# A two-layer hybrid encoder on one core: attention values of all heads in one 512-column set, and a new order of the units and gates around them

## The chip, the cores and the metric

The kernel runs on one NeuronCore of a Trainium2 chip. The core has a matrix engine (TensorE, PE in the profile, with its weight loads listed as PEld), a vector engine (VectorE, DVE), a scalar engine (ScalarE, ACT), GpSimd (POOL) and a sync engine (SP) that here only issues DMA transfers. Matrix products accumulate in PSUM banks of 128 partitions by 512 floats; all other data of the core is in SBUF. The metric is the device time of one execution in microseconds; before the change its median over three runs is 1792.9 us.

## The reference

The input `x` has 512 tokens of 1024 features. Each of two layers normalises `x` and projects it once, with `w_in`, into everything that three token mixers need:

```
h = rmsnorm(x, norm_mix[i])
qa, ka, va, glu_in, qc, kc, vc, gates = split(h @ w_in[i])
ya = diff_attention(qa, ka, va, ...)        # 4 heads, value width 128 each: va has 512 columns
yb = conformer_conv(glu_in, ...)            # a * sigmoid(g) over 512 channels, then 31 taps, layernorm, silu
yc = neighbourhood_attention(qc, kc, vc, rpb)  # 8 heads of 64: vc has 512 columns; 8x16 windows, bias
ga, gb, gc = split(sigmoid(gates))          # 3 x 1024 columns
x = x + (ga*(ya@w_br_a) + gb*(yb@w_br_b) + gc*(yc@w_br_c)) @ w_o
x = x + (silu(rmsnorm(x)@w_ffn_gate) * (rmsnorm(x)@w_ffn_up)) @ w_ffn_down
x = x + sigmoid(rmsnorm(x)@w_ple_gate) * (p[i] @ w_ple_in)
```

A last RMS norm follows both layers. The change lies in the first half of each layer, from the projection `h @ w_in` to the merge of the three branches.

## The kernel before

**Products.** All arithmetic of the matrix engine keeps float32 accuracy by splitting each operand into a high and a low half. A product is three matmuls: high weights by high activations (L177), high weights by low activations (L178), low weights by high activations (L179). A weight block of 128 by 1024 floats (512 KB) is loaded by SP into a tile `wr`; ScalarE copies its high half into `wh` (L143) and VectorE subtracts to get the low half `wl` (L157). There are three buffers each of `wr`, `wh` and `wl`, so a block can be split only when the block three before it has been used up. A gemm (`gemm`, `proj`) multiplies one block with the eight 128-feature slices of the activations: 24 matmuls of 512 columns into one PSUM bank. PSUM is shared out as three banks `mm` for gemms, two `sc` for scores, two `tr` for transposes and one `av` for attention outputs.

**Order.** The program order of PE is written out by hand. VectorE, ScalarE and SP work through orders that the scheduler makes from priorities; each executes its own list strictly in order. Inside the hand order a small clock spreads the attention work: each product of three matmuls is a *chunk*, four chunks (12 matmuls of 512 columns) make one *stretch* (`tick`), and `later(unit, delay, gap)` starts an attention unit at the earliest `delay` stretches after now and leaves at least `gap` stretches to the next one. A unit runs in steps: its scores, two stretches later its transposes, two stretches later its products with the values, whose result is read out of the bank `av` by ScalarE and VectorE (the tiles `natten_y` for the neighbourhood attention, and the like for the differential one).

**The stage of the change.** In a layer the gemms follow as: the convolution's gated units (four pairs of a value and a gate, `glu`); neighbourhood pairs 0 to 3, each a Q and a K gemm (`natten_in`) and four units; their values (`natten_v`), a first half after pair 0 and a second half after pair 2; differential heads 0 to 3 (`diff_in`) with their values (`diff_v`) in two halves; the gates of the neighbourhood branch (`gate_c`, eight gemms, the first of them behind head 1) and two of the gates of the convolution branch (`gate_b`); the sigmoid of these ten in one block (one table load on ScalarE); then `branch_c`, two more `gate_b` and `merge_a`. In layer 0 the first gemms use activations that are not normalised yet (their result is scaled by the norm afterwards); `renorm` meanwhile writes normalised activations `hs` (the tiles `glu_h<-pre_x`, each a high half on ScalarE and a low half on VectorE, L160), and everything from the first values on uses these.

**The values.** Values come out with tokens on the partitions: 128 tokens of the activations are the stationary operand, the weights are streamed through. `values` before the change does one half of the heads: 256 columns, eight feature slices, four token tiles, three matmuls each (L572, L574, L576), which makes 96 matmuls of 256 columns into two `mm` banks with two weight blocks.

**Background work.** The 31 taps of the convolution for each of four channel tiles are single VectorE operations (`conv_z<-glu_z,pre_par,conv_z`, L160, the first of a tile L505). They are dealt out behind other work in numbers set by the table `BG` (for instance four behind each sigmoid of `merge_a`, and two behind each sum, `mergea2`).

## Time and profile before

| what | us |
|---|---|
| median of three runs | 1792.9 |
| the runs | 1792.49, 1792.9, 1795.68 |
| profiled execution, whole | 1793.18 |
| profiled execution, span of the core | 1791.4 |
| PE busy in the span | 1777.5 (99%) |
| DVE busy in the span | 1381.7 (77%) |
| ACT busy in the span | 894.0 (50%) |

The profile is of one execution. The span is the time between its first and its last instruction; 1.8 us of the execution lie around it. A line of the timeline gives start, duration, engine, source line, operation, the tile written and those read, the shape, a count, and in square brackets the time that the engine sat idle before, with what ended it. The durations of matmuls are modelled latencies that overlap, so the pace of PE is read from the starts, not from the durations. Tile names carry the stage in which they were allocated: `natten` is the neighbourhood attention, `diff` the differential one, `glu_h` the activations, `gatec`/`gateb` the gates.

### The profile page before, as it was taken

The numbers are of one execution on the slowest core, as the hardware profiler recorded it, in microseconds if no ns is written. First come the engines' busy times: TensorE is split into PE (matmuls) and PEld (weight loads), VectorE is DVE, ScalarE is ACT, GpSimd is POOL, SyncE is SP. The second block draws the span as 40 slices with busy tenths as digits, with TensorE's granted clock in tenths as the row PEclk, the third lists the DMA queues.
The fourth block names the chain that finished last, engine by engine and source line by source line (L and its number), as shares of the span: only waits on it lengthen the run. The fifth ranks groups of instructions, "written<-read, shape, count | busy, mean of one in ns | idle before, by whom it ended". The sixth has DMA issues, their size and how long they took to land. (4 is left out here: it accounts for less than half of the span.)

```text
span 1791.4 us, 27360 instructions
## 1 busy us (share of the span) xinstructions
PE 1777.5 (99%) x10404; PEld 1571.6 (88%) x10404; DVE 1381.7 (77%) x2140; ACT 894.0 (50%) x1497; POOL 63.5 (4%) x102
## 2 busy tenths in 40 slices
PE   9999999999999999999999999999999999999998
PEld 7888888888899899898878888888888998998987
DVE  7888887897877577577787878878878775765776
ACT  5466555325565245255545755553256652542544
POOL 0000000000000000000000000000000100000000
PEclk9999999999999999999999999999999999999999
DMA  5666561335646456253437655523364662663432
GB/s 200 174 185 169 143 163 43 102 89 167 209 143 186 140 150 195 79 139 121 159 117 191 187 152 160 130 63 103 98 190 148 194 178 84 190 179 111 116 109 95
DMA packets 98387, 257.56 MB, mean 144 GB/s; under 512 B 12880, under 2 KB 17616, under 8 KB 98256
## 3 DMA queue, kind: packets, MB, share of 16 engines
q1 hardware_dynamic: 90912, 231.00, 41.5%
q0 software_dynamic: 6336, 23.07, 7.1%
q8 instruction: 82, 1.34, 0.3%
q10 hardware_dynamic: 1008, 1.75, 0.3%
q14 instruction: 49, 0.40, 0.1%
HBM read 216.44 MB, written 7.86 MB: 125 GB/s over the span
## 5 line engine op out<-in xcount | busy, mean ns | idle before, releaser
L143 ACT ACTIVATE ffn_wh<-ffn_wr 128x1024 fp32r<-128x1024 f32 (+1 forms) x114 | 117.3, 1029 | 184.2 <-PE ffn_mm L178 104.4
L160 DVE SCALAR_TENSOR_TENSOR conv_z<-glu_z,pre_par,conv_z 128x512 f32<-128x512 f32 x240 | 179.1, 746 | 2.9
L157 DVE TENSOR_TENSOR ffn_wl<-ffn_wr,ffn_wh 128x1024 fp32r<-128x1024 f32 (+1 forms) x114 | 134.9, 1183 | 45.0 <-ACT ffn_wh L143 44.6
L1047 PE MATMUL ffn_sc<-wo_h,ffn_wh 128*128 128x256 f32 x704 | 130.4, 283 | 0.0
L1047 PEld LDWEIGHTS ffn_sc<-wo_h,ffn_wh 128*128 128x128 f32 x704 | 110.4, 192 | 0.8
L1047 PE MATMUL ffn_sc<-wo_h,ffn_wl 128*128 128x256 f32 x352 | 99.6, 283 | 0.0
L177 PE MATMUL ffn_mm<-ffn_z,ffn_wh 128*128 128x512 f32 x240 | 93.5, 389 | 0.0
L178 PE MATMUL ffn_mm<-ffn_z,ffn_wh 128*128 128x512 f32 x240 | 93.4, 389 | 0.0
L179 PE MATMUL ffn_mm<-ffn_z,ffn_wl 128*128 128x512 f32 x240 | 93.4, 389 | 0.0
L157 DVE TENSOR_TENSOR ffn_t<-ffn_mm,wo_r 128x512 f32<-128x512 f32 x48 | 33.0, 688 | 73.9 <-PE ffn_mm L179 73.8
L157 DVE TENSOR_TENSOR ffn_wl<-ffn_rp,ffn_wh 128x1024 fp32r<-128x1024 f32 x44 | 53.7, 1221 | 30.1 <-ACT ffn_wh L143 30.1
L143 ACT ACTIVATE mergea_wh<-mergea_wr 128x1024 fp32r<-128x1024 f32 (+1 forms) x32 | 27.1, 846 | 96.8 <-PE mergea_mm L178 70.8
L1047 PEld LDWEIGHTS ffn_sc<-wo_h,ffn_wl 128*128 128x128 f32 x352 | 67.5, 192 | 0.0
L1047 PE MATMUL ffn_sc<-wo_qk,ffn_wh 128*128 128x256 f32 x352 | 67.1, 283 | 0.0
L1047 PE MATMUL ffn_sc<-wo_v,ffn_wh 128*128 128x256 f32 x352 | 67.1, 283 | 0.0
L1047 PE MATMUL ffn_av<-wo_h,ffn_wh 128*128 128x256 f32 x352 | 65.3, 283 | 0.0
L143 ACT ACTIVATE ffn_wh<-ffn_rp 128x1024 fp32r<-128x1024 f32 x44 | 46.4, 1055 | 29.3 <-PE ffn_mm L178 17.5
L1047 PEld LDWEIGHTS ffn_sc<-wo_qk,ffn_wh 128*128 128x128 f32 x352 | 54.9, 192 | 0.0
L1047 PEld LDWEIGHTS ffn_av<-wo_h,ffn_wh 128*128 128x128 f32 x352 | 54.9, 192 | 0.0
L1047 PEld LDWEIGHTS ffn_sc<-wo_v,ffn_wh 128*128 128x128 f32 x352 | 54.9, 192 | 0.0
L179 PEld LDWEIGHTS ffn_mm<-ffn_z,ffn_wl 128*128 128x128 f32 x240 | 45.0, 188 | 9.4
L177 PEld LDWEIGHTS ffn_mm<-ffn_z,ffn_wh 128*128 128x128 f32 x240 | 45.1, 188 | 9.2
(674 smaller groups left out, 5779.6 us busy)
## 6 DMA issues: line engine op xcount, KB each, us to landing
ffn_wr<-w_gu SPq DMA_DIRECT2D x66, 512.0 KB, 4.2
ffn_e<-w_gu SPq DMA_DIRECT2D x32, 512.0 KB, 3.3
ffn_e<-w_gu POOLq DMA_DIRECT2D x32, 512.0 KB, 7.9
ffn_wr<-w_fd SPq DMA_DIRECT2D x32, 512.0 KB, 4.5
natten_wr<-w_in SPq DMA_DIRECT2D x16, 512.0 KB, 3.9
natten_b<-bias SPq DMA_DIRECT2D x32, 256.0 KB, 2.9
diff_wr<-w_in SPq DMA_DIRECT2D x16, 512.0 KB, 3.7
gatec_wr<-w_in SPq DMA_DIRECT2D x16, 512.0 KB, 4.2
```

Of the source, the lines that this page charges most:

```text
L143: i = self.nc.scalar.activation(out, in_, func, **kw)
L157: return self.nc.vector.tensor_tensor(out, a, b, op)
L160: return self.nc.vector.scalar_tensor_tensor(out, a, s, b, op0, op1)
L177: mm(out, wh, ah, start=first, stop=False)
L178: mm(out, wh, al, start=False, stop=False)
L179: mm(out, wl, ah, start=False, stop=last)
L1047: mm(bank[:, u], w[:, u, kp], t, start=begin and n == 0, stop=False, skip_group_check=True)
```

## The change

The two calls of `values` for each attention become one, for all heads: 96 matmuls of 512 columns (L591, L592, L593 in the new numbering) with four weight blocks. Four token tiles then need four PSUM banks. Three come from `mm`; the fourth is the bank `av`, and it is taken up after 36 matmuls, by doing the first four feature slices of tiles 0 to 2 ahead of tile 3. The fourth weight block reuses the buffers of the first, which is in use up to the 42nd matmul; the 55th matmul is the first that needs the fourth block. The results go to VectorE and ScalarE one token tile at a time.

Around that, the order is new. The fourth pair of gated units (`glu_last`) moves from ahead of neighbourhood pair 0 to behind pair 1; its two gemms are copied out by ScalarE, its sigmoid joins the block of the gates' sigmoids, and the product (`finish`) follows then. Neighbourhood units are at least two stretches apart, not one, with a delay of six stretches for pair 0 and of four for the others, not five. Gate gemms now stand between the neighbourhood pairs and the differential heads and between these heads; all four `gate_b` stand ahead of the sigmoid block, so that 13 sigmoids follow in a row, not ten, and `merge_a` follows directly on `branch_c`. The delays of the differential units are 8, 6, 6 and 7 stretches for heads 0 to 3, with a gap of one for the last head. In layer 0 the pairs of gated units and neighbourhood pair 0 no longer have taps behind them; `mergea2` deals out three taps, not two. The copies of the values' edges for the other half of the rows go to four tiles of the tag `t`, not to one of the tag `x`, and four gate tiles get buffers of the tags `b`, `rp` and `v`. The host's layout of the two value weights (`_vblocks`) follows.

```
-BG = dict(glu=2, natten=3, diff=1, gatec=2, branchc=1, gateb=5, mergea=4, mergea2=2)
+BG = dict(glu=2, natten=3, diff=1, gatec=2, branchc=1, gateb=5, mergea=4, mergea2=3)
...
-        self.glu(zs)
+        self.glu(zs, range(3))
...
         self.natten_in(0, sn, yc)
         self.drain(self.renorm)
         self.h = self.hs
-        self.natten_v(0, sn)
+        self.natten_v(sn)
         self.natten_in(1, sn, yc)
+        finish = self.glu_last(zs)
         self.natten_in(2, sn, yc)
-        self.natten_v(1, sn)
+        self.gates(acc, gb, "cc")
         self.natten_in(3, sn, yc)
-        acc, gb = [], []
+        self.gates(acc, gb, "c")
         self.diff_in(0, sd, ya)
-        self.diff_v(0, sd)
+        self.gates(acc, gb, "c")
         self.diff_in(1, sd, ya)
-        self.gate_c(acc, 0)
+        self.diff_v(sd)
         self.diff_in(2, sd, ya)
-        self.diff_v(1, sd)
+        self.gates(acc, gb, "bb")
         self.diff_in(3, sd, ya)
-        for m in range(1, KD):
-            self.gate_c(acc, m)
-        for m in range(2):
-            self.gate_b(gb, m, AF.Copy, None)
+        self.gates(acc, gb, "ccbbcc")
         for g in acc + gb:
             self.act(g, g, AF.Sigmoid, table="sigmoid")
+        finish()
         self.branch_c(acc, yc)
-        for m in range(2, 4):
-            self.gate_b(gb, m, AF.Sigmoid, "sigmoid")
         self.merge_a(ya, acc)
...
+                zc = self.gated(z, ta, sg)
-                if j:
+                if j and self.i:
                     self.background(zc, self.bg["glu"])
...
+    def glu_last(self, zs):
+
+        self.phase = "glu"
+        sg = self.sb("r", [P, 512])
+        z = self.sb("z", [P, GW + 2 * HALO, GR])
+        zs.append(z)
+        mid = z[:, HALO:HALO + GW, :].rearrange("p a b -> p (a b)")
+        for out, off in ((sg, CB), (mid, 0)):
+            self.act(out, self.proj(OFF_GLU + off + 3 * P), AF.Copy)
+
+        def finish():
+            self.act(sg, sg, AF.Sigmoid, table="sigmoid")
+            self.gated(z, mid, sg)
+
+        return finish
...
-        accs = [self.ps("mm", (P, 2, 256)) for _ in range(2)]
-        for o in range(0, KD, 4):
-            wh, wl = self.weights(ap[:, o * 256:(o + 4) * 256], 1024)
-            for k in range(o, o + 4):
...
+        accs = [self.ps("mm") for _ in range(3)]
+        ws = []
+
+        def products(t, ks):
+            ts = slice(t * P, (t + 1) * P)
+            for k in ks:
+                wh, wl = ws[k // 2]
+                s = slice(k % 2 * 512, k % 2 * 512 + 512)
+                hi, lo = self.halves(self.h[k])
+                mm(accs[t], hi[:, ts], wh[:, s], start=k == 0, stop=False)
+                mm(accs[t], hi[:, ts], wl[:, s], start=False, stop=False)
+                mm(accs[t], lo[:, ts], wh[:, s], start=False, stop=k == KD - 1)
                 self.chunk()
-                self.chunk()
+
+        for o in range(4):
+            ws.append(self.weights(ap[:, o * 1024:(o + 1) * 1024], 1024))
+        for t in range(3):
+            products(t, range(2))
+        for t in range(3):
+            products(t, range(2, 4))
+        accs.append(self.ps("av"))
+        products(3, range(4))
         vs = []
-        for acc in accs:
+        for t in range(4):
+            products(t, range(4, KD))
             v = self.sb("v", [P, 2, 512], F32R)
...
-            self.later(self.natten_unit(pr, n // 2, n % 2, st4, k2, st, box, ys[pr]), 5, 1)
+            self.later(self.natten_unit(pr, n // 2, n % 2, st4, k2, st, box, ys[pr]),
+                       4 if pr else 6, 2)
...
-            self.later(self.diff_unit(head, qt, st4, k2, st, box, ys), 6 if head else 7, 2)
+            self.later(self.diff_unit(head, qt, st4, k2, st, box, ys), (8, 6, 6, 7)[head],
+                       1 if head == 3 else 2)
...
+    def gates(self, acc, gb, names):
+        for n in names:
+            if n == "c":
+                self.gate_c(acc, next(self.ms[0]))
+            else:
+                self.gate_b(gb, next(self.ms[1]), AF.Copy, None)
```

The first place to follow in the order is PE at the start of the first set of values in layer 0, behind the K gemm of neighbourhood pair 0. Before:

```order
L572 MATMUL natten_mm_120_634<-natten_wh_123_637,glu_h_78_381 128x256
L574 MATMUL natten_mm_120_634<-natten_wl_124_638,glu_h_78_381 128x256
L576 MATMUL natten_mm_120_634<-natten_wh_123_637,glu_h_78_381 128x256
L572 MATMUL natten_mm_120_634<-natten_wh_123_637,glu_h_78_381 128x256
L574 MATMUL natten_mm_120_634<-natten_wl_124_638,glu_h_78_381 128x256
L576 MATMUL natten_mm_120_634<-natten_wh_123_637,glu_h_78_381 128x256
L572 MATMUL natten_mm_121_635<-natten_wh_123_637,glu_h_78_381 128x256
L574 MATMUL natten_mm_121_635<-natten_wl_124_638,glu_h_78_381 128x256
L576 MATMUL natten_mm_121_635<-natten_wh_123_637,glu_h_78_381 128x256
L572 MATMUL natten_mm_121_635<-natten_wh_123_637,glu_h_78_381 128x256
```

After:

```order
L591 MATMUL natten_mm_108_548<-natten_wh_112_552,glu_h_77_378 128x512
L592 MATMUL natten_mm_108_548<-natten_wl_113_553,glu_h_77_378 128x512
L593 MATMUL natten_mm_108_548<-natten_wh_112_552,glu_h_77_378 128x512
L591 MATMUL natten_mm_108_548<-natten_wh_112_552,glu_h_82_403 128x512
L592 MATMUL natten_mm_108_548<-natten_wl_113_553,glu_h_82_403 128x512
L593 MATMUL natten_mm_108_548<-natten_wh_112_552,glu_h_82_403 128x512
L591 MATMUL natten_mm_109_549<-natten_wh_112_552,glu_h_77_378 128x512
L592 MATMUL natten_mm_109_549<-natten_wl_113_553,glu_h_77_378 128x512
L593 MATMUL natten_mm_109_549<-natten_wh_112_552,glu_h_77_378 128x512
```

Each matmul now has 512 columns, and a feature slice of one token tile is followed by the next slice of the same tile (`glu_h_77` and `glu_h_82` are slices 0 and 1); the second and third bank come after 6 and 12 matmuls.

The second place is VectorE in layer 0, where it reads the Q and the K bank of neighbourhood pair 0 out of PSUM (`natten_t<-natten_mm`). Before:

```order
L397 TENSOR_REDUCE glu_lam_102_528<-glu_t_101_526 128x4
L157 TENSOR_TENSOR pre_x_18_84<-pre_x_18_84,glu_r_76_347 128x512
L160 SCALAR_TENSOR_TENSOR natten_t_113_576<-natten_mm_108_541,glu_r_76_347 128x512
L160 SCALAR_TENSOR_TENSOR natten_t_118_618<-natten_mm_114_587,glu_r_76_347 128x512
L157 TENSOR_TENSOR glu_nlam_103_531<-glu_lam_102_528 128x2
L404 TENSOR_SCALAR glu_nlam_103_531<-glu_nlam_103_531 128x1 x2
L157 TENSOR_TENSOR natten_wl_137_773<-natten_wr_135_771,natten_wh_136_772 128x1024
L160 SCALAR_TENSOR_TENSOR glu_h_112_561<-pre_x_18_84,pre_par_1_67,glu_h_112_561 128x512
L160 SCALAR_TENSOR_TENSOR natten_t_113_576<-natten_t_113_576,natten_kh_107_540 128x512
```

After (here `natten_t_105<-natten_mm_99` is the K bank):

```order
L157 TENSOR_TENSOR pre_x_18_84<-pre_x_18_84,glu_r_76_347 128x512
L404 TENSOR_SCALAR glu_nlam_87_435<-glu_nlam_87_435 128x1 x2
L160 SCALAR_TENSOR_TENSOR natten_t_98_484<-natten_t_98_484,natten_kh_91_444 128x512
L157 TENSOR_TENSOR natten_wl_119_565<-natten_wr_117_563,natten_wh_118_564 128x1024
L160 SCALAR_TENSOR_TENSOR glu_h_103_512<-pre_x_17_83,pre_par_1_67,glu_h_103_512 128x512
L160 SCALAR_TENSOR_TENSOR glu_h_104_528<-pre_x_18_84,pre_par_1_67,glu_h_104_528 128x512
L160 SCALAR_TENSOR_TENSOR natten_t_105_531<-natten_mm_99_492,glu_r_76_347 128x512
L157 TENSOR_TENSOR pre_x_18_84<-pre_x_18_84,glu_r_76_347 128x512
L160 SCALAR_TENSOR_TENSOR natten_t_105_531<-natten_t_105_531,natten_kh_91_444 128x512
L160 SCALAR_TENSOR_TENSOR glu_h_107_545<-pre_x_18_84,pre_par_1_67,glu_h_107_545 128x512
```

Before, Q and K bank were read out one after the other, with the normalised activations but one written ahead of them. Now the K bank's row stands behind a weight split (`natten_wl`) and two writes of activations (`glu_h_103`, `glu_h_104`), which the values also need.

The third place is VectorE at the last neighbourhood units of layer 0, where it reads out the bank `av` (`natten_y<-natten_av`). Before:

```order
L157 TENSOR_TENSOR natten_y_287_1583<-natten_av_360_1991,natten_y_287_1583 64x256
L157 TENSOR_TENSOR natten_pt_368_2041<-natten_tr_365_2033,natten_pt_368_2041 128x512
L157 TENSOR_TENSOR natten_y_287_1583<-natten_y_287_1583,natten_av_360_1991 64x256
L157 TENSOR_TENSOR natten_a_367_2035<-natten_tr_366_2034,natten_a_367_2035 64x128
L157 TENSOR_TENSOR natten_y_287_1583<-natten_av_374_2081,natten_y_287_1583 64x256
L852 TENSOR_REDUCE diff_s_375_2090<-diff_sc_376_2091 128x1
L157 TENSOR_TENSOR natten_y_287_1583<-natten_y_287_1583,natten_av_374_2081 64x256
L852 TENSOR_REDUCE diff_s_375_2090<-diff_sc_378_2097 128x1
L857 RECIPROCAL diff_s_375_2090<-diff_s_375_2090 128x1
```

After:

```order
L895 TENSOR_REDUCE diff_s_400_2070<-diff_sc_401_2071 128x1
L157 TENSOR_TENSOR diff_rp_383_1990<-diff_rp_383_1990,diff_r_308_1589 128x512
L160 SCALAR_TENSOR_TENSOR conv_z_164_830<-glu_z_64_316,pre_par_1_67,conv_z_164_830 128x512
L157 TENSOR_TENSOR diff_rp_383_1990<-diff_rp_383_1990,diff_r_309_1591 128x512
L157 TENSOR_TENSOR natten_y_293_1514<-natten_y_293_1514,natten_av_378_1968 64x256
L157 TENSOR_TENSOR diff_rp_383_1990<-diff_rp_383_1990 128x512
L895 TENSOR_REDUCE diff_s_400_2070<-diff_sc_403_2077 128x1
L157 TENSOR_TENSOR diff_rp_383_1990<-diff_rp_383_1990,diff_kh_359_1850 128x512
L900 RECIPROCAL diff_s_400_2070<-diff_s_400_2070 128x1
L160 SCALAR_TENSOR_TENSOR diff_s_400_2070<-diff_s_400_2070,glu_nlam_87_435,diff_sm_342_1773 128x1
L160 SCALAR_TENSOR_TENSOR diff_a_402_2075<-diff_e_404_2081,diff_s_400_2070,diff_a_402_2075 128x512
L157 TENSOR_TENSOR diff_wl_399_2034<-diff_wr_397_2032,diff_wh_398_2033 128x1024
```

Before, the two parts of a read-out (a difference that writes `natten_y` from `natten_av`, and a sum that adds to it) have one row between them, a unit's transposes or a softmax sum of the differential heads (L852). The rows after begin right behind the difference of the last unit: now four more rows come ahead of its sum, a softmax sum (L895), two rows of the differential heads' rotary embedding (`diff_rp`) and a tap of the convolution (`conv_z`). The last row is the split of the fourth weight block of the differential values (`diff_wl_399`); it stands behind the softmax of a differential unit (L900, `diff_a`).

More of the change, by code (lines that the diff above doesn't have):

```diff
@@ L461, in proj, with glu @@
         return ps
-    def glu(self, zs):
+    def glu(self, zs, js):
         self.phase = "glu"
-        if not self.first:
+        if 0 in js and not self.first:
             self.first = [self.ps("mm") for _ in range(2)]
             self.pair(self.first, [self.a["w_in"][self.i, (OFF_GLU + o) // P] for o in (CB, 0)], self.h)
-        nc = self.nc
-        for j in range(4):
+        for j in js:
             sg, ta = self.sb("t", [P, 512]), self.sb("t", [P, 512])
@@ L693, in natten_unit @@
         yield 2
-        vs, vd = st["v", pr // 2]
+        vs, vds = st["v"]
+        g = pr // 2
         if u == 0:
```

77 lines of the change are left out of this document (39 added, 38 removed).

## The prediction

> **What bounds the kernel now.** I read the page first, then the waits of PE, then the busy time of the changed stage by engine, and last the timelines around the places that the change moves. The page says which engine sets the time:
>
> ```profile
> PE 1777.5 (99%) x10404; PEld 1571.6 (88%) x10404; DVE 1381.7 (77%) x2140; ACT 894.0 (50%) x1497; POOL 63.5 (4%) x102
> PEclk9999999999999999999999999999999999999999
> ```
>
> PE is busy for 1777.5 of 1791.4 us, and its granted clock is full in every slice, so nothing here is a matter of the clock. A change can gain only in two ways: fewer or cheaper matmuls, or fewer of the 13.9 us in which PE idles. It loses by whatever makes PE wait. The waits of PE, with total, number and longest, in us:
>
> ```profile
> PE natten_av L702 <- DVE natten_y L157: 1.9, 3, 1.2
> PE natten_tr L681 <- DVE natten_pt L157: 1.3, 2, 0.7
> PE pre_av L325 <- DVE pre_zeror L378: 1.1, 1, 1.1
> PE ple_tr L213 <- DVE ple_ss L157: 1.0, 1, 1.0
> PE natten_sc L760 <- DMA natten_x<-natten_t: 0.9, 1, 0.9
> PE natten_sc L760 <- issue: 0.6, 1, 0.6
> ```
>
> Four of the six rows are the neighbourhood attention's: 1.9 + 1.3 + 0.9 + 0.6 = 4.7 us in seven waits. The stage from the K and Q gemms of pair 0 to the branch merge, once for each layer:
>
> ```profile
> 51.12:341.80 290.68, 286.78 (x1633) 248.78 (x1632) 240.62 (x473) 163.47 (x357) 7.62 (x19) 1.00 0.52 145
> 939.30:1227.40 288.10, 286.73 (x1634) 248.71 (x1633) 235.09 (x457) 160.04 (x352) 7.50 (x19) 1.00 0.53 145
> ```
>
> After the length come PE, PEld, DVE and ACT. PE idles 3.90 us in layer 0 and 1.37 us in layer 1; DVE works 240.62 of 290.68 us, 83%, so it has room on average and its order decides.
>
> **Term 1: the width of the value matmuls.** The pace of PE is read from starts:
>
> ```profile
> 51.12 0.39 PE L177 MATMUL natten_mm<-glu_v,natten_wh 128*128 128x512 f32 x1
> ...
> 62.08 0.28 PE L572 MATMUL natten_mm<-natten_wh,glu_h 128*128 128x256 f32 x1
> ...
> 73.46 0.28 PE L576 MATMUL natten_mm<-natten_wh,glu_h 128*128 128x256 f32 x1
> 73.58 0.40 PE L177 MATMUL natten_mm<-glu_h,natten_wh 128*128 128x512 f32 x1
> ```
>
> From 51.12 to 62.08 there are 48 matmuls of 512 columns without a wait: 10.96 us, 0.2283 us each. From 62.08 to 73.58 there are 96 of 256 columns: 11.50 us, 0.1198 us each. A set of both halves costs 192 x 0.1198 = 23.00 us before and 96 x 0.2283 = 21.92 us after, 1.08 us less; two attentions in two layers make four sets, **-4.3 us**. The new matmul has 128 tokens as stationary operand and weights of 512 columns streaming; its nearest row is the gemm's at equal shape and type, whose operands are only exchanged. The ends: nothing, if a wide matmul cost two narrow ones, and -4.3.
>
> The Trainium skill, page "TensorE: Matmul & The Clock Gate", section "Wait — 56ns, not 53.3ns?", puts back-to-back matmuls at N / 2.4 GHz plus about 2.5 ns. By that, an estimate from the page, 768 narrow ones cost 83.9 us and 384 wide ones 82.8 us, a gain of only 1.0 us, and the sum below would come out 3.3 us higher. The trace here disagrees: both of its paces lie 13 to 15 ns above N / 2.4 GHz, and the measured fixed part decides what merging two into one saves.
>
> **Term 2: the neighbourhood units' waits.** Before, with a gap of one stretch, a unit's values follow a unit's that has not been read out:
>
> ```profile
> 100.16 0.39 PE L179 MATMUL natten_mm<-glu_h,natten_wl 128*128 128x512 f32 x1
> 101.76 0.71 PE L702 MATMUL natten_av<-natten_pt,natten_v 128*128 128x256 f32 x4 [1.21 <-DVE natten_y L157]
> ...
> 105.66 0.71 PE L702 MATMUL natten_av<-natten_pt,natten_v 128*128 128x256 f32 x4 [0.33 <-DVE natten_y L157]
> ```
>
> From 100.16 to 101.76 there are 1.60 us where 0.23 would do, so the wait costs 1.37 us where the table gives 1.21: 0.16 us more. With seven waits the whole is 4.7 + 7 x 0.16 = 5.8 us. Two stretches between units are 24 gemm matmuls, 5.5 us, against 2.7 before; and the read-out is a copy on ACT and two operations on DVE:
>
> ```profile
> L143 ACT ACTIVATE natten_y<-natten_av x32: 362/378/382, 93.4 to 1070.7; 64x256 fp32r<-64x256 f32 x32
> L157 DVE TENSOR_TENSOR natten_y<-natten_av,natten_y x32: 394/422/429, 93.9 to 1075.2; 64x256 fp32r<-64x256 f32 x32
> L157 DVE TENSOR_TENSOR natten_y<-natten_y,natten_av x32: 416/420/425, 95.0 to 1076.4; 64x256 fp32r<-64x256 f32 x32
> ```
>
> That is 1.2 us of work, and even with four DVE operations of 0.7 us in between it ends within 4.1 us, so the waits on `natten_y` and `natten_pt` go. The wait of scores on a transfer is one of SP's order:
>
> ```profile
> 78.36 0.36 PE L760 MATMUL natten_sc<-natten_x,natten_qk 128*128 128x256 f32 x1 [0.88 <-DMA natten_x<-natten_t]
> ```
>
> ```profile
> 70.42 0.34 SPq L171 DMA_DIRECT2D natten_wr<-w_vc  x1
> 70.81 1.67 SPq L619 DMA_DIRECT2D natten_x<-natten_kh  x2
> 72.52 1.24 SPq L619 DMA_DIRECT2D natten_qk<-natten_t  x2
> 73.80 1.24 SPq L619 DMA_DIRECT2D natten_x<-natten_t  x2
> ```
>
> SP held these copies behind a weight load that had to wait for its buffer until 70.42, and the last was issued at 73.80 to 75.04. After the change pair 0's units start six stretches, 16.5 us, after its K gemm, and the two more weight loads of the longer set take SP about 0.34 us each. This wait and the 0.6 us next to it go: **-5.8 us**. The ends are -5.8 and -2.9 (half of them come back elsewhere). Every unit now occupies PE's order for longer, and the differential heads start later; that costs PE nothing as long as gemms stand between, which the order gives by putting gates there.
>
> **Term 3: the third bank in layer 0.** The first values now start at 51.12, right behind the K gemm; they need their third bank 12 matmuls later, at 51.12 + 2.74 = 53.86. That bank held K, and DVE has to read it out, standing in its new order behind a weight split and two activation writes. DVE in this stretch before:
>
> ```profile
> 32.73 1.89 DVE L157 TENSOR_TENSOR glu_t<-pre_mm,glu_r 128x512 f32<-128x512 f32 x3 [2.94 <-ACT glu_r L143]
> ...
> 58.97 0.74 DVE L160 SCALAR_TENSOR_TENSOR conv_z<-glu_z,pre_par,conv_z 128x512 f32<-128x512 f32 x1
> 59.63 0.42 DVE L157 TENSOR_TENSOR glu_t<-glu_t 128x256 f32<-128x256 f32 x1
> ...
> 60.96 0.68 DVE L157 TENSOR_TENSOR pre_x<-pre_x,glu_r 128x512 f32<-128x512 f32 x1
> 61.56 1.41 DVE L160 SCALAR_TENSOR_TENSOR natten_t<-natten_mm,glu_r 128x512 f32<-128x512 f32 x2
> 62.88 0.15 DVE L157 TENSOR_TENSOR glu_nlam<-glu_lam 128x2 f32<-128x2 f32 x1
> 63.07 0.21 DVE L404 TENSOR_SCALAR glu_nlam<-glu_nlam 128x1 f32<-128x1 f32 x2
> 63.20 1.22 DVE L157 TENSOR_TENSOR natten_wl<-natten_wr,natten_wh 128x1024 fp32r<-128x1024 f32 x1
> ```
>
> From 32.73 on DVE sits idle for 0.3 us until 62.88, when both banks are out. Ahead of K's read-out the new order leaves out six conv taps (0.66 us each from 58.97 to 59.63, the first at 0.5), the fourth pair of gated units (some 2.2 us) and one weight split (1.14), and adds 0.7 for the small `glu_nlam` rows. 62.9 - 3.8 - 2.2 - 1.1 + 0.7 gives 56.5; adding up row by row from 37.17 on gives 55.9. Against 53.86 that is 2.0 to 2.6 us: **+2.2 us**, once. The ends: 0, if DVE's earlier rows run faster than I add up, and 3. In layer 1 the activations are ready and DVE is waiting for work there, so the bank is read out at once:
>
> ```profile
> 939.44 0.69 DVE L157 TENSOR_TENSOR glu_t<-glu_mm,ple_r 128x512 f32<-128x512 f32 x1 [3.35 <-PE glu_mm L179]
> ```
>
> **Term 4: the fourth bank and the fourth block.** The bank `av` must be free after 36 matmuls. At the differential values the last neighbourhood unit has just used it: four score matmuls and 12 products lie between, 16 x 0.2283 = 3.65 us. In that time come ACT's copy (0.38), two DVE rows (0.42 each) and four rows between them: 0.6, 0.6, 0.66 and 0.6 by the starts above. That is 3.7 us, about even; I take 0.3 us in each layer, between 0 and 1. The fourth weight block can be split only after the 42nd matmul, and is needed by the 55th (high) and 56th (low), 2.74 and 2.97 us later. The same chain before is this, with the DVE row at 63.20 above:
>
> ```profile
> 62.09 1.06 ACT L143 ACTIVATE natten_wh<-natten_wr 128x1024 fp32r<-128x1024 f32 x1 [0.81 <-PE natten_mm L178]
> ```
>
> PE's release at 62.08 leads to a low half at 64.42, 2.34 us. So 0.6 us are to spare and I cost it at nothing. The cover is thin: in the differential sets the split stands on DVE behind the softmax of a unit. What is queued behind it on DVE are transposes and read-outs whose next user is at least a stretch away.
>
> **Term 5: gates and merge.** The gate gemms and the fourth gated pair only change places: zero PE time. The sigmoids now number 13:
>
> ```profile
> 300.09 1.28 ACT L143 ACT_TABLE_LOAD   x1
> 301.38 4.28 ACT L143 ACTIVATE gatec_x<-gatec_x 128x512 f32<-128x512 f32 x8
> ```
>
> Each takes 0.535 us, three more are 1.6 us ahead of whatever ACT copies next for the last differential units; the gemms in front of it (three banks) give 5.5 us or more. I take 0.4 us in each layer, between 0 and 1.5. In `merge_a` the third tap behind each sum adds 0.66 us per step to DVE:
>
> ```profile
> 342.00:407.00 65.00, 65.00 (x288) 53.81 (x288) 58.37 (x79) 18.03 (x26) 0.00 (x0) 1.00 0.31 92
> ```
>
> 58.37 + 8 x 0.66 = 63.7 of 65.0 us: DVE stays just under PE's pace, and three `mm` banks buffer it. The taps that layer 0 no longer does early end up here. I cost it at nothing; its cover is 1.3 us per layer. Terms 4 and 5 together: 2 x 0.3 + 2 x 0.4 = **+1.4 us**, with ends 0 and 5.
>
> **Sum.** 1793.18 - 4.3 - 5.8 + 2.2 + 1.4 = 1786.7 on the profiled execution. That one is 0.28 us above the median of the runs, so the forecast is **1786.4 us**. Without any new wait it would be 1782.8.
>
> **Rivals.** *B, the waits move rather than go:* the third bank is late in both layers (+2.2) and half of the neighbourhood waits persist (+2.9): 1786.4 + 5.1 = 1791.5. For it speaks that DVE is 83% busy and its order now mixes three kinds of work; against it the 3.35 us idle row of layer 1 and the doubled distance. *C, slower: the fourth weight block is split too late.* One mechanism, in all four sets: if DVE comes to the split q us after ACT has done the high half, PE waits q - 0.6 us each time. To lose 10.1 us and so end above 1796.5, q has to be 3.1 us, about five DVE operations in front. For it speaks the place of the split behind a softmax; against it the row at 63.20, which follows the high half at once on a DVE that is busy throughout. *D, the wide matmul saves nothing:* if a 512-column matmul with weights streaming took two narrow ones, 0.2396 us, term 1 is zero: 1790.7. The equal shape at 51.12 speaks against it.
>
> **How the numbers follow.** A difference of 0.2%, 3.6 us, is about what a measurement of this kernel can tell from no change: faster means below 1789.3, slower above 1796.5. The forecast's own case, with its terms anywhere between their ends, holds 0.70 and lies below 1789.3. B holds 0.15 and D 0.03, both within 0.2%; C holds 0.12. The low end, 1781.5, is the case without new waits, 1782.8, with 1.3 us off for the small waits in other places of the table; the high end, 1791.5, is B. C lies outside.
>
> **What would show it.** PE's waits without `natten_av`, `natten_tr` and `natten_sc` confirm term 2; L591 to L593, 384 matmuls at a pace of 0.228 us, term 1; a wait of about 2 us of L591 on DVE `natten_t` in layer 0 alone, term 3; no wait on `wl` inside L591 to L593, and small ones on the bank `av` and after the sigmoids, terms 4 and 5. The prediction is wrong if the units' read-outs still end late behind the heads' rotary rows, or if `wl` appears as a releaser in each set.

## The result, and the profile after

The changed kernel takes 1797.28 us (median of 18 runs) against 1794.28 us for the kernel before (18 runs beside it): a ratio of 1.0023, 95% interval 1.0016 to 1.003. By the ratio it is slower by about 4 us (the medians differ by 3.0 us), where 6.5 us less were forecast. Small as this is, it is the difference of a gain that came and a loss that was larger. The engines after, and the waits of PE (total, number, longest):

```profile
PE 1773.8 (99%) x10020; PEld 1553.7 (86%) x10020; DVE 1372.2 (76%) x2112; ACT 897.9 (50%) x1481; POOL 63.5 (4%) x102
```

```profile
PE natten_tr L710 <- ACT natten_e L143: 5.1, 2, 2.5
PE diff_sc L798 <- ACT diff_a L143: 2.3, 2, 1.2
PE natten_mm L591 <- DVE natten_t L160: 1.7, 1, 1.7
PE natten_tr L708 <- ACT natten_e L143: 1.6, 2, 0.8
PE diff_av L591 <- DVE natten_y L157: 1.5, 2, 0.7
...
PE diff_av L177 <- DVE diff_v L157: 0.9, 2, 0.5
...
PE natten_av L731 <- DVE natten_a L157: 0.4, 2, 0.2
PE conv_tr L556 <- DVE conv_qk L157: 0.2, 1, 0.2
PE conv_tr L556 <- ACT conv_qk L143: 0.2, 1, 0.2
```

384 matmuls fewer, and the neighbourhood waits of before are gone: no row has `natten_y` as the releaser of `natten_av`, none a DMA. In their place stand 13.9 us of new waits. PE idles for 22.4 us of the span, not 13.9, and is busy for 3.7 us less: 4.8 us in all. The new waits lie where the change worked; this table gives the starts of the first matmuls of some stages in the timeline of PE:

| stretch of PE | before | after | difference |
|---|---|---|---|
| start to `merge_a` of layer 0 | 341.84 | 343.79 | +1.95 |
| last gates to `merge_b`, layer 0 | 31.34 | 32.42 | +1.08 |
| `merge_b` of layer 0 to `glu` of layer 1 | 454.90 | 454.90 | 0 |
| `glu` to `merge_a`, layer 1 | 334.01 | 336.25 | +2.24 |
| last gates to `merge_b`, layer 1 | 29.27 | 29.27 | 0 |

The rest of the kernel behind it is 0.5 us shorter.

The largest wait, in layer 0 (layer 1 has the same one 889 us later), on PE:

```profile
173.23 0.30 PE L731 MATMUL natten_av<-natten_a,natten_t 128*128 128x128 f32 x1 [0.21 <-DVE natten_a L157]
176.06 0.90 PE L710 MATMUL natten_tr<-pre_ident,natten_e 128*128 128x128 f32 x4 [2.53 <-ACT natten_e L143]
...
177.38 0.39 PE L177 MATMUL diff_mm<-glu_h,diff_wh 128*128 128x512 f32 x1
177.61 0.52 PE L178 MATMUL diff_mm<-glu_h,diff_wh 128*128 128x512 f32 x1
177.93 0.63 PE L179 MATMUL diff_mm<-glu_h,diff_wl 128*128 128x512 f32 x1
178.35 0.63 PE L177 MATMUL diff_mm<-glu_h,diff_wh 128*128 128x512 f32 x1
```

The transposes of the second unit of neighbourhood pair 3 wait for ScalarE's exponential `natten_e`. And behind the wait there is something that no part of the prediction held: matmuls of 512 columns that start 0.42 to 0.43 us apart, not 0.23. Seven of them here and six in layer 1 last 0.63 us, or 0.41 us with 256 columns. The trace's record of the granted clock has it too: half the clock for 3.41 us from 177.73 in layer 0, and for 3.41 us from 1065.19 in layer 1. A line of this view gives a stretch, its length, then busy time and number of instructions of PE, PEld, DVE, ACT and POOL, then the granted clock, the share of the DMA engines and GB/s:

```profile
174.31:177.73 3.42, 1.62 (x11) 1.38 (x12) 3.21 (x7) 2.78 (x8) 0.15 (x1) 1.00 0.77 195
177.73:181.14 3.41, 3.41 (x10) 2.63 (x9) 3.32 (x10) 1.63 (x5) 0.00 (x0) 0.50 0.33 123
```

With PE busy all through, 3.41 us at half the clock do the work of 1.7 us.

### The profile page after: what moved, and what is told of

Read it like the earlier page. It is cut to its first block, busy times and chain, and to the rows that moved or that the text cites. A ratio compares the mean times of both kernels' runs of the same rounds, so it can differ in the third digit from the quotient of the medians.

```text
span 1796.2 us, 26565 instructions
## 1 busy us (share of the span) xinstructions
PE 1773.8 (99%) x10020; PEld 1553.7 (86%) x10020; DVE 1372.2 (76%) x2112; ACT 897.9 (50%) x1481; POOL 63.5 (4%) x102
## 4 chain that ended last, share of the span: by engine, by line
PE 93%; DVE 4%; ACT 1%; issue 1%; DMA 0%; POOL 0%; POOLq 0%; DVEq 0%; ACTq 0%
PE ffn_sc L1090 14%; PE ffn_av L1090 7%; PE ffn_mm L178 4%; PE ffn_mm L177 4%; PE ffn_mm L179 4%; PE ffn_tr L1090 4%; PE mergea_mm L177 2%; PE mergea_mm L178 2%; PE mergea_mm L179 2%; PE gatec_mm L178 2%; PE gatec_mm L179 2%; PE gatec_mm L177 2%; PE wo_mm L177 2%; PE wo_mm L178 2%; PE wo_mm L179 2%; PE diff_sc L798 2%
## 5 line engine op out<-in xcount | busy, mean ns | idle before, releaser
L143 ACT ACTIVATE natten_e<-natten_b,natten_s 128x256 f32<-128x256 f32 x64 | 32.2, 503 | 47.0 <-issue 42.8
```

The source lines that it names most:

```text
L143: i = self.nc.scalar.activation(out, in_, func, **kw)
```

## The experiments

The releaser named is ScalarE, but what is late is one step further back, on VectorE:

```profile
166.72 1.23 DVE L157 TENSOR_TENSOR diff_wl<-diff_wr,diff_wh 128x1024 fp32r<-128x1024 f32 x1 [1.92 <-PE natten_sc L798]
167.86 0.68 DVE L157 TENSOR_TENSOR diff_rp<-diff_rp,diff_r 128x512 f32<-128x512 f32 x1
168.46 0.75 DVE L160 SCALAR_TENSOR_TENSOR conv_z<-glu_z,pre_par,conv_z 128x512 f32<-128x512 f32 x1
...
172.79 0.29 DVE L157 TENSOR_TENSOR natten_a<-natten_tr,natten_a 64x128 fp32r<-64x128 f32 x1
173.11 0.42 DVE L684 CUSTOM_DVE_ANT_0 natten_b<-natten_sc,natten_b 128x256 f32<-128x256 f32 x1
```

The unit's scores were done at about 167; its softmax row (L684) stands on DVE behind a weight split, the rotary rows of differential head 0 (`diff_rp`), a tap, and another unit's read-out and transposes, ten rows in all, and starts at 173.11. So theory A: the order of DVE's rows makes the new waits. Rivals: ScalarE is late by itself, or the spacing of the units is wrong; and for the slow matmuls, that they belong to the place and not to the wait. All results, each as a ratio to the kernel before on the same chip:

| kernel | ratio, 95% interval | median, us | span of the profile, us |
|---|---|---|---|
| after | 1.0023 (1.0016 to 1.0030) | 1797.28 | 1796.2 |
| softmax rows first | 0.9986 (0.9976 to 0.9995) | 1790.34 | 1788.7 |
| head 3 at gap two | 1.0041 (1.0026 to 1.0056) | 1801.01 | 1797.1 |
| filled wait | 1.0038 (1.0025 to 1.0051) | 1800.59 | 1798.2 |
| K bank first | 1.0005 (0.9996 to 1.0014) | 1794.51 | 1791.5 |
| wide neighbourhood values alone | 1.0139 (1.0111 to 1.0167) | 1820.57 | 1821.2 |
| taps as before | 1.0062 (1.0045 to 1.0079) | 1804.01 | 1801.3 |
| pair 3 at gap one | 1.0050 (1.0033 to 1.0067) | 1802.22 | 1802.2 |
| four kinds of rows first | 0.9970 (0.9959 to 0.9982) | 1787.85 | 1786.1 |
| three kinds first, taps moved | 0.9960 (0.9948 to 0.9973) | 1786.16 | 1784.4 |
| before, rows first | 0.9992 (0.9981 to 1.0002) | 1791.62 | 1790.6 |
| three kinds first, with probes | 1.0164 (1.0135 to 1.0194) | 1822.83 | 1822.1 |

### Softmax rows first

```
-            nc.vector.tensor_tensor_reduce(
+            with self.tc.high_priority(offset=100): nc.vector.tensor_tensor_reduce(
```

> Only VectorE's order changes: the softmax row of a neighbourhood unit (L684) is taken as soon as its scores are there, ahead of the rotary rows of differential head 0. Theory A, the transposes of pair 3's first units wait because L684 stands behind these rotary rows: the waits of L710 and L708 on natten_e (2.53 and 0.79 us in each layer) go, and with the long one the stretch of matmuls at 0.43 us behind it; 2 x (2.53 + 0.79) + 1.4 + 0.9 = about 9 us less than after, some 1788 us. Rival B, ScalarE is late with the exponentials, or the units stand too close, whatever VectorE does: natten_tr waits of over 1.5 us remain and the time stays within 2 us of after.

Theory A holds. VectorE takes the unit's softmax row ahead of the rotary rows:

```profile
165.59 1.22 DVE L157 TENSOR_TENSOR diff_wl<-diff_wr,diff_wh 128x1024 fp32r<-128x1024 f32 x1 [3.23 <-ACT diff_wh L143]
166.73 0.41 DVE L684 CUSTOM_DVE_ANT_0 natten_b<-natten_sc,natten_b 128x256 f32<-128x256 f32 x1
```

```profile
PE natten_tr L710 <- ACT natten_e L143: 2.3, 4, 0.7
```

6.7 us on `natten_e` became 2.3, in four waits of at most 0.7 us, and the granted clock is full from 6.3 us to the end of the work. The span falls by 7.5 us and the ratio by 0.37%, 6.6 us. This alone turns the slower kernel into a faster one. What is left is mostly VectorE's order again: the next row of the same softmax, the reciprocal (L696), was not moved and still stands behind the rotary rows, and ScalarE waits for it:

```profile
172.67 0.17 DVE L696 RECIPROCAL natten_s<-natten_s 128x2 f32<-128x2 f32 x1
172.93 0.91 ACT L143 ACTIVATE natten_e<-natten_e,natten_s 128x256 f32<-128x256 f32 x2 [0.34 <-DVE natten_s L696]
```

Only the longer wait of layer 0, 0.72 us at 182.05, has a share of ScalarE's own: the copy of a weight block's high half, 1.04 us from 180.55, stands between its two scalings of `natten_e`. That much of rival B holds.

### Units of pair 3 closer together

```
-                       4 if pr else 6, 2)
+                       4 if pr else 6, 1 if pr == 3 else 2)
```

> After, with the units of neighbourhood pair 3 one stretch apart, as before, and those of the other pairs two apart. If the waits on natten_e come from units of pair 3 that last into the gemms and rotary rows of differential head 0, they shrink from 3.3 us in each layer to under 1 us, and the natten_av and natten_pt waits of closely spaced units come back in their place with 0.5 to 1.5 us in each layer: 3 to 6 us less than after. Rival: the first unit of pair 3 meets the rotary rows whatever the spacing: its 2.5 us stay, and the time is after's within 2 us.

The expected gain of 3 to 6 us is refuted: the kernel is 0.27% slower still.

```profile
PE natten_tr L710 <- DVE natten_pt L157: 4.7, 2, 2.4
PE natten_av L730 <- DVE natten_y L157: 3.0, 2, 1.6
```

Waits of the same size come at the same place under another name, and the waits of before (`natten_av` on `natten_y`) return on top. For pair 3 the spacing isn't the cause: its units meet the rotary rows either way, and what counts is who comes first on VectorE. The other pairs kept their gap of two, so this run says nothing on theirs.

### Head 3 at gap two

```
-                       1 if head == 3 else 2)
+                       2)
```

> The units of differential head 3 two stretches apart, as the other heads' are, in place of one. If the gap of one is what makes the scores wait for ScalarE's read of their bank (1.16 us by the table, 1.32 us by starts, in each layer), that wait goes and the time falls by 2.6 us. Rival: the last unit, three stretches later, is then late for the merge, and a wait on its result of some 1 to 3 us at branch_c or merge_a takes its place, so that the time stays or rises.

The wait on `diff_a` goes, as the gap of one stretch says, but the rival holds in kind, at another place:

```profile
PE diff_tr L852 <- DVE diff_a L160: 3.9, 2, 1.9
```

The later units' transposes now wait for VectorE. In the changed kernel the wait on `diff_a` itself is again a chain through both engines: on VectorE the maximum of the scores stands behind a tap, and on ScalarE the read of the bank behind a weight split that is blocked until PE frees a buffer:

```profile
297.33 0.74 DVE L160 SCALAR_TENSOR_TENSOR conv_z<-glu_z,pre_par,conv_z 128x512 f32<-128x512 f32 x1
297.99 1.28 DVE L895 TENSOR_REDUCE diff_s<-diff_sc 128x1 f32<-128x512 f32 x2
```

```profile
298.62 0.63 ACT L143 ACTIVATE branchc_wh<-branchc_wr 128x512 fp32r<-128x512 f32 x1 [2.70 <-PE gateb_mm L178]
299.16 0.67 ACT L143 ACTIVATE diff_a<-diff_sc,diff_s 128x512 f32<-128x512 f32 x1
```

The scores were done at about 296. Which of the two alone would be enough was not separated. With head 3 at gap two the kernel is no faster: a ratio of 1.0041 against 1.0023, with intervals that overlap.

### K bank first

```
-                self.stt(t, ps, f, self.rb, ALU.mult, ALU.mult)
+                with self.tc.high_priority(offset=200): self.stt(t, ps, f, self.rb, ALU.mult, ALU.mult)
```

> In layer 0 VectorE reads out the K bank of neighbourhood pair 0 ahead of a weight split and two writes of activations, five rows or 3.2 us earlier in its order. If the third bank is what L591 waits for, the wait on natten_t (1.66 us by the table, 1.82 us by starts) goes and 1.8 us with it; the rest of the trace is unchanged. Rival: the rows pushed back (the third weight block's low half, two activations) are then late themselves and a wait of 1 to 2 us on natten_wl or glu_h appears a little later in the same set: no gain.

The wait of L591 on `natten_t` is gone from the table, and none on `natten_wl` or `glu_h` has come. The ratio falls by 0.18%, 3.2 us, more than 1.8 but, at intervals of some 1.5 us to either side, not clearly more. (In the one profiled execution the stretch at half the clock in layer 1 is absent too; whether this edit has to do with that is not shown.) The third bank is confirmed as this wait's cause.

### Taps as before

```
-BG = dict(..., mergea=4, mergea2=3)
+BG = dict(..., mergea=4, mergea2=2)
...
-                if j and self.i:
+                if j:
...
-                            self.bg["natten"] if pr or self.i else 0)
+                            self.bg["natten"])
```

> After, with the background taps as before: those of layer 0 behind the gated pairs and behind neighbourhood pair 0, and two, not three, behind each sum of merge_a. Theory: the 1.1 us that the stretch between merge_a and merge_b of layer 0 has grown by (31.34 to 32.42 us, waits of conv_tr on conv_qk) come from taps that end later, and go; in return the third bank's wait (1.66 us) grows by the taps ahead of it, 5 x 0.66, to 4 or 5 us. Net some 2 us slower than after. Rival: the conv waits come from the later fourth gated unit, whose taps can't start before the sigmoid block: they stay, and only the third bank's wait grows.

Both halves of the theory hold: from the last gates to `merge_b` of layer 0 it is 31.41 us again, and the third bank pays:

```profile
PE natten_mm L591 <- DVE natten_t L160: 6.2, 1, 6.2
```

Seven taps now stand ahead of the K bank, some 4.4 us by their starts, and the wait is 4.5 us longer. So leaving them out early was worth more than the 1.1 us that they cost at the end. The wait's length was 6.2 us, not 4 to 5, and the loss is 5.1 us in the span, not 2: behind this wait the clock is at half from 57.02 to 63.85, of which 4.1 us fall on matmuls.

### Wide neighbourhood values alone

The kernel before, with this in place of its two calls (the layout of `w_vc` and the indices in `natten_unit` follow):

```
-        self.natten_v(0, sn)
+        self.natten_v(sn)
...
-        self.natten_v(1, sn)
```

> The kernel before, with one part of the change alone: the values of the neighbourhood attention in one set of 512 columns with four weight blocks, directly behind pair 0 (the call behind pair 2 goes); the differential values, the order, the spacing and the gates stay as before. If merging two narrow matmuls into a wide one is worth 1.08 us per set, as the pace of PE says, the set from its first to its last matmul takes 21.9 us against 23.0 and the kernel is about 2.2 us faster than before, with the waits of before. Rival: the longer set needs a fourth bank and a weight block that comes late, or starves the units behind it, and new waits of 2 us or more eat it: same or slower than before.

The rival is right and far too modest: 1.4% slower than before, 25 us.

```profile
PE natten_sc L797 <- DMA natten_x<-natten_t: 6.8, 1, 6.8
PE natten_av L739 <- DVE natten_y L157: 4.3, 6, 1.3
PE diff_mm L177 <- ACT diff_rp L143: 4.1, 2, 2.0
PE natten_av L739 <- DVE natten_v L157: 3.5, 2, 1.8
```

The last copies of the scores' operands stand behind two weight loads in SP's queue; they are issued at 75.65, when PE is there, and land 6.5 to 6.7 us later (before: 4.3 to 4.4 us). Units then reach their values before these are split, and the clock is at half in seven stretches. The width of the matmul is not in question: in the set, 59 steps from 61.76 to 75.16 take 0.2271 us each. A wider set in the old order is a loss, so it needed some new order around it. The new order with the narrow matmuls was not run, so what it is worth by itself is open.

### Four kinds of rows first

The edits of "Softmax rows first" and "K bank first", and in the same way the sum that ends a neighbourhood unit and the maximum of the differential scores:

```
-        self.tt(y[rs, 1, qs], y[rs, 1, qs].bitcast(F32), av[ro], ALU.add)
+        with self.tc.high_priority(offset=100): self.tt(y[rs, 1, qs], y[rs, 1, qs].bitcast(F32), av[ro], ALU.add)
...
-            nc.vector.tensor_reduce(out=m[:, u:u + 1], in_=sc, op=ALU.max, axis=AX.X, negate=True)
+            with self.tc.high_priority(offset=100): nc.vector.tensor_reduce(out=m[:, u:u + 1], in_=sc, op=ALU.max, axis=AX.X, negate=True)
```

> After, with four kinds of VectorE rows taken earlier in its order and nothing else changed: the softmax rows of the neighbourhood units (L684), the read-out of the K bank of pair 0, the sum that ends a neighbourhood unit (and frees the bank av), and the maximum of differential scores (L895). If every new wait is one of VectorE's order, it removes those on natten_e (6.7 us with 2.3 us of slow matmuls), natten_t (1.8), the bank av (1.8) and diff_a (2.6): 9 + 1.8 + 1.8 + 2.6 = 15 us less than after at most, about 1782 us. If the one on diff_a is ScalarE's (its read stands behind a weight split that waits for PE), that one stays: about 1785 us.

The waits on `natten_t`, on the bank `av` and on `diff_a` are all gone. For the last the edit names VectorE's row alone, but in the trace ScalarE's read of the bank (292.22) has come ahead of the weight split (293.77) as well, so the two are still not separated. And the early maximum pushes other rows of the heads back:

```profile
PE diff_tr L226 <- DVE diff_pt L157: 2.7, 2, 1.4
...
PE diff_tr L852 <- DVE diff_sm L215: 0.9, 1, 0.9
```

3.6 us come for 2.3 that go, and 2.3 us on `natten_e` stay. 10 us less than after in the span, not 15.

### Three kinds first, taps moved

Without the maximum, and with the taps of `merge_a` dealt out earlier:

```
-BG = dict(..., gatec=2, ..., mergea2=3)
+BG = dict(..., gatec=3, ..., mergea2=2)
```

> After, with the three earlier kinds of rows that free a bank or feed a transpose (softmax rows L684, the read-out of the K bank, the sum that ends a unit), not the maximum of the differential scores; and with three taps behind each gate_c and two behind each sum of merge_a, so that the taps of layer 0 end earlier. Theory: the waits of conv_tr on conv_qk go (1.1 us in layer 0), the diff_sc waits (2.3 us) stay and the diff_tr waits on diff_pt and diff_sm (3.6 us), which the early maximum brought in, go: 1 to 3 us less than best_a, about 1786 us. Rival: the third tap behind each gate delays rows that PE waits for in the gates' stretches, and natten_tr or diff_tr waits grow by more than 1.1 us.

The theory holds: no wait on `conv_qk`, 31.34 us from the last gates to `merge_b` as before, no wait of `diff_tr`; `diff_sc` on `diff_a` is 2.8 us. At 1786.16 us and a ratio of 0.9960 this beats both kernels, by 0.4% and 0.6%. Against the four kinds the ratio's interval overlaps; the span is 1.7 us shorter.

### Before, rows first

The softmax rows and the closing sums of the units taken earlier, without the K bank, in the kernel before.

> The kernel before, with its neighbourhood units' softmax rows and closing sums taken earlier by VectorE, and nothing of the change. If these rows' place in the order is worth as much to any arrangement, it removes the 1.9 and 1.3 us of waits on natten_y and natten_pt and gains some 3 to 4 us against before, so that the change's own gain over it is small. If the waits of before come from units that follow each other at one stretch, whose read-out follows its products however the rows are sorted, under 1.5 us are gained: same as before.

```profile
PE natten_av L702 <- DVE natten_y L157: 2.1, 7, 0.5
```

The single waits become smaller and more, and the ratio can't be told from 1. So these two kinds of rows bring nothing that can be told from noise without the change. That it is the mixing of units and heads which makes their place matter is argued, not shown.

### The filled wait and the clock

```
+        for _ in range(10 if pr == 3 and (half, u) == (0, 0) else 0):
+            mm(pt, self.ones_r, self.halves(self.h[0])[0], start=True, stop=True)
         for t, (e, _) in enumerate(es):
```

> After, with 10 matmuls of 512 columns whose result nobody reads, put into the 2.5 us in which TensorE waits ahead of the transposes of pair 3's first unit, in both layers; nothing else is changed and the transposes wait for the same data. Theory: the 7 and the 3 matmuls at 0.43 us behind this wait run at the half clock because TensorE had idled for 2.5 us; with the wait filled they run at 0.23 us and the span is 1.4 + 0.9 = 2.3 us shorter although 20 matmuls are added. Rival: they are slow for what they are (first rows of a gemm, its operands, transfers at that time): the slow matmuls stay, and the span is the same or longer.

This missed. The unit that waits at 176.06 is the second of pair 3, and the added matmuls stand ahead of the first one's transposes; the wait stayed, now at the third unit:

```profile
186.17 0.33 PE L710 MATMUL natten_tr<-pre_ident,natten_e 128*128 128x128 f32 x1 [2.83 <-ACT natten_e L143]
```

The slow stretch of layer 0 was absent here behind this wait, and present in layer 1 behind one of the same length. So the length of a wait alone does not decide. To test the wait as the cause, waits were made on purpose, in the fastest kernel, in each `merge_a`, after gates 0, 2, 4 and 6 (n = 1, 2, 4, 6):

```
...
+                with self.tc.high_priority(offset=300):
+                    p = self.ps("tr")
+                    mm(p, self.ones_r, hi, start=True, stop=True)
+                    s = self.sb("t", [P, 512], F32R)
+                    self.act(s, p, AF.Copy)
+                    for _ in range(n - 1):
+                        self.act(s, s.bitcast(F32), AF.Copy)
+                    q = self.ps("tr")
+                    mm(q, self.ones_r, s, start=True, stop=True)
```

> The kernel best_d, which has no slow matmuls, with four probes in the merge_a of each layer, where TensorE otherwise has no wait at all: one matmul, then 1, 2, 4 or 6 copies of its result by ScalarE one after the other, then a matmul that reads the last copy, so that TensorE waits for some 0.8, 1.4, 2.6 and 3.8 us in the middle of full work. Their results go nowhere. Theory: a wait of over about 2 us itself brings on a stretch at the half clock: behind the longer two probes some 5 to 8 matmuls start 0.43 us apart, in at least half of the cases, and behind the shorter two none. Rival: the slow stretches belong to the place (gemms of the differential head at a time of many transfers): none appears in merge_a, however long the wait.

The probes in layer 0; layer 1 has waits of 1.17, 1.83, 3.16 and 4.53 us:

```profile
346.79 0.50 PE L775 MATMUL mergea_tr<-mergea_t,pre_onesr 128*128 128x512 f32 x1 [1.17 <-ACT mergea_t L143]
...
365.69 0.50 PE L775 MATMUL mergea_tr<-mergea_t,pre_onesr 128*128 128x512 f32 x1 [1.83 <-ACT mergea_t L143]
...
385.93 0.80 PE L775 MATMUL mergea_tr<-mergea_t,pre_onesr 128*128 128x512 f32 x1 [3.16 <-ACT mergea_t L143]
...
410.39 0.80 PE L775 MATMUL mergea_tr<-mergea_t,pre_onesr 128*128 128x512 f32 x1 [4.48 <-ACT mergea_t L143]
```

| wait, us | slow matmuls behind it, layer 0 | layer 1 |
|---|---|---|
| 1.17 | 0 | 0 |
| 1.83 | 0 | 8 |
| 3.16 | 13 | 6 |
| 4.48, 4.53 | 11 | 7 |

The place is not the cause; the wait is. One point of the theory was off: a wait of 1.83 us, behind which none was expected, brought it on in one of two cases; what tells the two apart stands in the last section. A matmul of 512 columns at 0.427 us costs 0.2 us more, so these stretches cost 1.2 to 2.6 us beyond the wait. The Trainium skill, page "TensorE: Matmul & The Clock Gate", section "HAM oscillation — how this bites in real kernels", gives as a rule that TensorE should not idle for more than about 3.4 us. The direction agrees; here half the clock came after waits of 1.83 and 2.53 us already, and the measurement decides.

## Why the prediction was wrong

The forecast was 1786.4 us and faster; it was slower, outside the range. As ratios, 0.9964 was forecast and 1.0023 measured, a miss of 10.6 us; the one line of "Softmax rows first" wins back 6.6 of them. By the terms:

- **Term 1, the width, was right.** In a stretch of the first set without other work, 53 steps take 12.04 us, 0.2272 each, against the 0.2283 used:

```profile
56.15 0.40 PE L592 MATMUL natten_mm<-natten_wl,glu_h 128*128 128x512 f32 x1
...
68.19 0.39 PE L591 MATMUL natten_mm<-natten_wh,glu_h 128*128 128x512 f32 x1
```

  Against 96 x 2 x 0.1198 us a set saves 1.2 us, 4.8 us for four sets. Rival D falls. The 1.0 us that the prediction estimated from the Trainium skill's page "TensorE: Matmul & The Clock Gate", section "Wait — 56ns, not 53.3ns?", is about a fifth of that (worked out again, its formula gives 83.8 and 82.9 us for the two kinds; the difference is 1.0 us all the same).
- **Term 2 failed, and it decided.** The waits it named did go (natten rows of before: 4.7 us, none left). The step that failed is its last one: later and longer units cost PE nothing "as long as gemms stand between". That looks at PE's order only. Gemms did stand between, and yet VectorE's order put a unit's softmax row behind ten others, the rotary rows of head 0 among them: 6.7 us of waits on `natten_e`, and stretches at half the clock behind the 2.53 us waits in both layers. The prediction came close in its own list of signs, where it names read-outs that end late behind the heads' rotary rows, but no term or rival had a price for it. Which part of the change put the row there (the spacing, the delays, the moved gates) stays open: before it, units of pair 3 also lie beside these rotary rows (scores done at 157.8, softmax row at 159.55), and PE does not wait. The half clock was not among the terms at all; the prediction's sentence that nothing here is a matter of the clock holds for the kernel before and its waits of at most 1.21 us.
- **Term 3 was right** in cause, place and layer: 1.66 us by the table and 1.8 by starts, against 2.2; putting the K bank's row earlier removed it.
- **Term 4** had the right cause and was sized too low: the bank `av` cost 0.74 us by the table in each layer, not 0.3; the first later use of the split values added 0.45. The fourth weight block never appears as a releaser, so rival C falls.
- **Term 5** was sized too low and put in the wrong place. What came was no wait on the 13 sigmoids, but 1.16 us in each layer on `diff_a`, from the units of head 3 at one stretch, whose gap no term priced (at two stretches it goes, and others come); and in layer 0 the taps that were costed at nothing ended late and cost 1.1 us ahead of `merge_b`. `merge_a` itself stayed at PE's pace, as said; the cover that mattered was that of the convolution behind it.
- **Rival B** named the right kind of loss, that waits move rather than go, but took its price from the waits of before. New waits of 6.7, 2.3 and 1.5 us at places that had none were not in it, and neither was what a wait of 2.5 us does to the clock.

That the fastest variant has a median of 1786.16 us, close to the 1786.4 us of the forecast, is luck. It lacks the third bank's 2.2 us, which the sum holds, its taps are dealt out otherwise, and it has 2.8 us of waits on `diff_a` and 2.3 us on `natten_e`, which the sum does not hold.

## What to carry to other kernels

When units of work are spread further apart on the engine that bounds the kernel, read in the order of the other engines what they now lie beside: a short row that releases the bounding engine may stand behind ten others, most of them not waited for yet. Such a row can be moved by a line of priority, which is worth trying before a spacing is retuned; two changes of spacing here only moved the wait. It is not free: the early maximum of the differential scores cost more waits than it saved. And a wait of some 2 us or more on TensorE should be priced with up to 1.7 us on top for every 3.41 us at half the clock that follow.

## What was not expected of the hardware

A wait of TensorE in the middle of full work brings on a stretch at half the clock. By the length of the wait alone it looks uncertain: among the probes it came behind none of two waits of 1.17 us, one of two of 1.83 us and four of four from 3.16 us on, but waits of 2.5 to 2.8 us passed without it three times (with the K bank first, with head 3 at gap two, with the filled wait).

The record of the granted clock tells these cases apart. The 13 traces hold 23 such stretches, not counting the program's first 7 us and its end. Each lasts 3.41 us or two or three times that, and within a trace all begin on one grid of 3.41 us. What goes ahead of one is idle time of TensorE in the single interval of this grid just before it, one wait or several. Of the intervals at full clock, those with 1.79 us of idle time or more were followed by half the clock in 18 of 18 cases, those with 1.56 to 1.77 us in 5 of 12, those with less in none. The probe's wait of 1.83 us was cut by the grid in layer 0 (0.94 and 0.89 us, the first two lines) and lay within one interval in layer 1 (the third line; the fourth follows it):

```profile
361.39:364.81 3.42, 2.47 (x11) 1.69 (x9) 3.07 (x5) 1.82 (x3) 0.00 (x0) 1.00 0.51 132
364.81:368.22 3.41, 2.52 (x11) 2.11 (x12) 3.41 (x6) 0.80 (x2) 0.00 (x0) 1.00 0.31 99
1265.93:1269.34 3.41, 1.57 (x7) 1.05 (x6) 3.10 (x5) 2.09 (x3) 0.00 (x0) 1.00 0.41 155
1269.34:1272.75 3.41, 3.41 (x9) 2.67 (x8) 2.25 (x4) 0.00 (x0) 0.00 (x0) 0.50 0.24 71
```

In the run with wide neighbourhood values alone, two waits of 0.58 and 0.98 us in one interval, 1.56 us together, were enough. This was read from the traces afterwards; no run moved a wait against the grid. The mean granted clock hardly shows a single stretch (0.998 over the changed kernel's profile), but over its 18 runs it goes with the time: the four runs at 0.996 took 1799.9 us on average, the four at 0.999 took 1796.3 us.
